# Mixture-of-experts stage: a fixed instruction order on three engines, weight splits four pieces ahead, thirteen packed positions

## The chip, the cores and the metric

One core of one Trainium2 chip runs the whole program in one launch. The metric is the device time of an execution in microseconds (us); less is better.

## What is computed

One layer of a decoder: attention and a convolution side by side, then a mixture of experts, both added to x, and a last norm. The change lies in the mixture of experts. Its core, for 1024 tokens of 1024 values, 32 experts, and two experts to each token:

```python
top_val, top_idx = lax.top_k(e_logits, TOP_K_INNER)
top_w = jax.nn.softmax(top_val, axis=-1) * p_grp[:, None]
...
return (jax.nn.silu(xblk @ w_gate[e]) * (xblk @ w_up[e])) @ w_down[e]
...
x = x + gt2 * hier_moe(h2, ...)
return rms_norm(x, g_final)
```

Everything is float32. Each expert has three weights, gate and up (1024 x 512) and down (512 x 1024), 2 MB each, so 192 MB of weights pass through the core once.

## The kernel before

**Stages.** The first 600 us compute attention, convolution, output projection and router. From about 604 us on, the experts are worked through in 32 positions. Positions 0 to LO-1 (LO = 6) hold the experts 0 to 5; the later positions are filled by the number of tokens of an expert, so that which expert stands at which position is known only when the router is done.

**Positions.** An ordinary position takes up to 128 tokens. A *packed* position (those in `PK`) takes an expert with at most 64 tokens. Position `XP` takes the expert with most tokens, in two blocks; the second is called position 32 (`E`), and each weight piece is used for both. Tokens beyond a position's capacity go to overflow blocks behind position 31, which are skipped when there are none, as here.

**One position.** A gather (L911, issued by GpSimd) fetches the rows of h from memory into one of NX = 3 buffers xe; TensorE transposes them (`stage_x`, L958, packed L949); gate and up follow (`stage_gu`), then a transpose of the hidden values (`stage_h`, L1012, packed L1006), then down (`stage_d`), a scaling on VectorE (packed L1040) and a scatter with addition into memory (L1023, GpSimd).

**Splits.** An ordinary position multiplies in a fast format and gets float32 accuracy from splitting both factors into a high and a low part. Each weight is cut into four pieces of 128 x 1024 values: ScalarE casts one to its high part (L924, ehi), VectorE subtracts (L925, elo), and TensorE does six matmuls (L990 to L992 for gate and up, L1056 to L1058 for down), 24 for a weight. A packed position takes the raw weight in float32 (L970, L1034) without a split. ehi and elo have three buffers each:

```python
hi = moe.tile([P, 2, 512], F32R, name="ehi", bufs=3)
lo = moe.tile([P, 2, 512], F32R, name="elo", bufs=3)
nc.scalar.copy(hi, src)
(nc.gpsimd if i == pool else nc.vector).tensor_tensor(lo, src, hi.bitcast(F32), op=OP.subtract)
```

**The weight stream.** SyncE loads every weight as two DMAs of 1 MB (L597) into a ring of eight slots of 2 MB, in the order of `uses`: gate of e, up of e, down of e-1. A load waits until the last reader of the weight eight places earlier is done. From position LO on, the expert's number is read from `pos` into a register of SyncE (L937) ahead of the first load of that position.

**Order of the work.** The program is written position by position: gate and up of e, transposes for e+1, down of e-1, transposes of e's hidden values. A scheduler of the language reorders the instructions within each engine. In program order the tables of the positions (`position_tables`, from L1097: which expert stands where, which tokens it has, their weights) stand behind position 1; the scheduler put them beside the gate of position 3.

```python
if e == LO - 5:
    position_tables()
```

Of the kernel before, what the change touches and what calls it, by code (L numbers as in the profile page):

```python
# [9 lines left out]
F32 = mybir.dt.float32  # L10
# [23 lines left out]
LO = 6  # L34
XP = 18
PK = (7, 9, 11, 13, 16, 17, 19, 20, 23, 25, 28, 31)
# [4 lines left out]
GUP = None  # L41
DP = None
# [3 lines left out]
def trunk_kernel(ctx, tc, x, c, w_mod, b_mod, g_norm1, w_in, conv_w, conv_b, conv_ln_g, conv_ln_b,  # L46
# [778 lines left out]
    uses = [u for e in range(E + 1) for u in ((e, 0), (e, 1), (e - 1, 2)) if 0 <= u[0] < E]  # L825
    wt = {}
# [32 lines left out]
    half_t = [rtc.tile([P, E - LO], dt, name=f"{nm}h") for nm, dt in (("ti", I32), ("ws", F32))]  # L859
# [8 lines left out]
    def tables(tb, dst, pool, halves=False):  # L868
# [8 lines left out]
        else:  # L877
# [28 lines left out]
    gat = []  # L906

    def gather(e):
        t = xe[len(gat) % NX]
        n = 2 if e in PK else 1  # L910
        i = nc.gpsimd.indirect_dma_start(  # L911
            out=t[:, 0:D // n], out_offset=None, in_=h2d.rearrange("t (n f) -> (t n) f", n=n),
            in_offset=bass.IndirectOffsetOnAxis(ap=slots(e)[0], axis=0),
            bounds_check=n * T - 1, oob_is_err=False)
        gat.append(i)
        return t

    def wparts(w, pool=None):

        for i in range(4):  # L920
            hi = moe.tile([P, 2, 512], F32R, name="ehi", bufs=3)
            lo = moe.tile([P, 2, 512], F32R, name="elo", bufs=3)
            src = w[:, 2 * i:2 * i + 2, :]
            nc.scalar.copy(hi, src)  # L924
            (nc.gpsimd if i == pool else nc.vector).tensor_tensor(lo, src, hi.bitcast(F32), op=OP.subtract)  # L925
            yield i, hi, lo

    st = {}

    expert = {}  # L930

    def stage_w(e):

        for u in uses[len(wt):3 * e + 2]:
            p, i = u
            if p >= LO and p not in expert:
                expert[p] = nc.values_load(pos[0:1, p:p + 1], engines=[mybir.EngineType.SP],  # L937
                                           min_val=0, max_val=E - 1)
            wt[u] = eload(wsrc(p, i, expert.get(p), p in PK))

    def stage_x(e):

        xt = st.pop(("g", e))
        if e in PK:

            x4 = moe.tile([P, 4, P], F32, name="x4", tag="xh")
            pt = psx.tile([P, 4, P], F32, name="pt")
            for j in range(4):
                nc.tensor.transpose(pt[:, j, :], xt[:, j:512:4], ident)  # L949
            nc.scalar.copy(x4, pt)  # L950
            st["x", e] = x4
            return
        xh = moe.tile([P, 8, P], F32R, name="xh")
        xl = moe.tile([P, 8, P], F32R, name="xl")
        for kk in range(2):
# [4 lines left out]
        st["x", e] = xh, xl  # L960

    def gu_halves(e):


        x4 = st.pop(("x", e))
        pg, pu = [psg.tile([P, F], F32, name=nm)[:, 0:256] for nm in ("pg", "pu")]
        for w, o in zip((wt[e, 0], wt[e, 1]), (pg, pu)):
            for k in range(8):
                for c in range(2):
                    nc.tensor.matmul(o[64 * c:64 * c + 64, :], x4[:, k % 4, k // 4 * 64:k // 4 * 64 + 64],  # L970
                                     w[:, k, 256 * c:256 * c + 256], start=(k == 0), stop=(k == 7),
                                     skip_group_check=True)
        hs = moe.tile([P, F], F32, name="hs")[:, 0:256]
        nc.scalar.activation(hs, pg, AF.Silu)
        nc.vector.tensor_mul(hs, hs, pu)
        st["h", e] = hs

    def stage_gu(*es):

        if es[0] in PK:  # L980
            return gu_halves(es[0])
        xs = [st.pop(("x", e)) for e in es]
        ps = []
        for w, nm in zip((wt[es[0], 0], wt[es[0], 1]), ("pg", "pu")):
            p = [psg.tile([P, F], F32, name=nm) for e in es]
            for i, hi, lo in wparts(w, GUP):
                for o, (xh, xl) in zip(p, xs):
                    for kk in range(2):
                        k = 2 * i + kk
                        nc.tensor.matmul(o, xh[:, k, :], hi[:, kk, :], start=(k == 0), stop=False)  # L990
                        nc.tensor.matmul(o, xh[:, k, :], lo[:, kk, :], start=False, stop=False)  # L991
                        nc.tensor.matmul(o, xl[:, k, :], hi[:, kk, :], start=False, stop=(k == 7))  # L992
            ps.append(p)
        for e, pg, pu in zip(es, *ps):
            hs = moe.tile([P, F], F32, name="hs")
            nc.scalar.activation(hs, pg, AF.Silu)
            nc.vector.tensor_mul(hs, hs, pu)
            st["h", e] = hs

    def stage_h(e):  # L1000
        hs = st.pop(("h", e))
        pt = psx.tile([P, 4, P], F32, name="pth")
        if e in PK:

# [3 lines left out]
            nc.scalar.copy(h2, pt[:, 0:2, :])  # L1008
            st["t", e] = h2
            return  # L1010
        for k in range(4):
            nc.tensor.transpose(pt[:, k, :], hs[:, k:F:4], ident)  # L1012
        if e == E:

            hh, hl = [moe.tile([P, 8, P], F32R, name=nm)[:, 0:4, :] for nm in ("xh", "xl")]
        else:
            hh, hl = [moe.tile([P, 4, P], F32R, name=nm, bufs=1) for nm in ("hh", "hl")]
        split(hh, hl, pt)
        st["t", e] = hh, hl

    def scatter(ys, e, n):
# [3 lines left out]
            out_offset=bass.IndirectOffsetOnAxis(ap=slots(e)[0], axis=0),  # L1025
            in_=ys, in_offset=None, bounds_check=n * T - 1, oob_is_err=False, compute_op=OP.add)

    def d_halves(e):
        h2 = st.pop(("t", e))
        wd = wt[e, 2].rearrange("p (k a) f -> p k (a f)", a=2)  # L1030
        py = psx.tile([P, D], F32, name="py")[:, 0:512]
        for k in range(4):
            for g in range(2):
                nc.tensor.matmul(py[64 * g:64 * g + 64, :], h2[:, k % 2, k // 2 * 64:k // 2 * 64 + 64],  # L1034
                                 wd[:, k, 512 * g:512 * g + 512], start=(k == 0), stop=(k == 3),
                                 skip_group_check=True)
        ys = moe.tile([P, D], F32, name="ys")[:, 0:512]
        for g in range(2):
            ps = slice(64 * g, 64 * g + 64)
            nc.vector.scalar_tensor_tensor(ys[ps], py[ps], slots(e)[1][ps], gt2b[ps, 512 * g:512 * g + 512],  # L1040
                                           op0=OP.mult, op1=OP.mult)
        scatter(ys, e, 2)

    def stage_d(*es):
        if es[0] in PK:
            return d_halves(es[0])
        hs = [st.pop(("t", e)) for e in es]
        wd = wt[es[0], 2]
        py = psx.tile([P, D], F32, name="py")
        py = [[py[:, 0:512], py[:, 512:1024]]]  # L1050
        if len(es) > 1:
            py.append([psg.tile([P, F], F32, name=nm) for nm in ("pg", "pu")])
        for k, hi, lo in wparts(wd, DP):
            for (hh, hl), o2 in zip(hs, py):
                for half, o in enumerate(o2):
# [3 lines left out]
        for e, o2 in zip(es, py):  # L1059
            ws = slots(e)[1]  # L1060
            ys = moe.tile([P, D], F32, name="ys")
            for half, o in enumerate(o2):
                sl = slice(half * 512, half * 512 + 512)
                nc.vector.scalar_tensor_tensor(ys[:, sl], o, ws, gt2b[:, sl], op0=OP.mult, op1=OP.mult)  # L1064
            scatter(ys, e, 1)

    def stage_g(e):
        st["g", e] = gather(e)


    order = [e for e in range(E) for e in ((e, E) if e == XP else (e,))]

    def next_x():

        n = nx[0]
        nx[0] += 1
        stage_x(order[n])
        if n + NX < len(order):
            stage_g(order[n + NX])

    nx = [0]

    def pth(p, n):
        return psx.tile([P, 512], F32, name="pth")[0:p, 0:n]
# [12 lines left out]
    def position_tables():  # L1097
# [5 lines left out]
        nc.tensor.matmul(pb, ones, Cc, start=True, stop=True)  # L1103
        kb = tmp(P, E)
        v.scalar_tensor_tensor(kb, pb, float(E), iota[:, 0:E], op0=OP.mult, op1=OP.add)
        pc = pth(E, 1)
        nc.tensor.matmul(pc, Cc, ones[:, 0:1], start=True, stop=True)
        cnt, kc, first, r = [tmp(E, 1) for i in range(4)]
        v.tensor_copy(cnt, pc)
        v.scalar_tensor_tensor(kc, cnt, float(E), tok1[0:E, 0:1], op0=OP.mult, op1=OP.add)  # L1110
        v.tensor_scalar(first, tok1[0:E, 0:1], LO + 0.5, float(P), op0=OP.is_lt, op1=OP.mult)
        m = tmp(E, n)
# [207 lines left out]
```

## Time and profile before

| | |
|---|---|
| median of three executions | 1221.63 us (1220.84 to 1222.86) |
| the profiled execution's own time | 1220.17 us |
| its span, first to last instruction | 1218.4 us |
| mean granted clock of TensorE | 0.952 |
| TensorE busy | 1099.1 us (90%) |
| VectorE busy | 809.3 us (66%) |
| ScalarE busy | 530.8 us (44%) |
| GpSimd busy | 216.4 us (18%) |
| moved by DMA | 292.65 MB, mean 240 GB/s |

The span is what the profile divides into stretches; the execution's own time has 1.8 us more around it. PE is TensorE, PEld its weight loads, DVE is VectorE, ACT ScalarE, POOL GpSimd, SP SyncE and SPq its DMA queue. Busy shares are means over stages that have different limits, so they are read by stretch. The granted clock is a share of TensorE's full clock; the DMA share is the mean busy share of the core's 16 DMA engines. In a group of instructions, x is their count, then come busy time and the mean in ns of one; what stands after the last bar or in brackets is the idle time in front of them, with what ended it.

### The profile page before, as it was taken

The page shows a single profiled execution, that of the slowest core. Times are in us where ns is not written, and L with a number is a line of the kernel's source. Part 1 is how long each engine was busy: PE and PEld are TensorE (multiplying, and loading weights), DVE is VectorE, ACT ScalarE, POOL GpSimd, SP SyncE. Part 2 cuts the span into 40 slices and gives each one's busy share as a digit, 9 for nine tenths or more (in the row PEclk, how much of TensorE's full clock was granted, in tenths as well). Part 3 has the DMA queues.
Part 4 walks back from the last instruction along what each step waited for, and adds up shares of the span by engine and source line. Part 5 has one row for each costly group of instructions (what it writes and reads, how often), then busy time and mean ns, then how long its engine had stood idle before and what let it go on. Part 6 is the DMA issues. An engine that isn't in the chain of part 4 may idle for free. (4 is left out here: it accounts for less than half of the span.)

```text
span 1218.4 us, 15998 instructions
## 1 busy us (share of the span) xinstructions
PE 1099.1 (90%) x5838; PEld 801.9 (66%) x5838; DVE 809.3 (66%) x1320; ACT 530.8 (44%) x809; POOL 216.4 (18%) x205
## 2 busy tenths in 40 slices
PE   4899999998999999999499999999989999999950
PEld 0667777786566666888377787777757666666630
DVE  1458999993664657776588997666743476576633
ACT  2431111114676753332276776555533354464513
POOL 2340000005221105001400222221220112111012
PEclk8799999999998999999699999999999999999985
DMA  9542634202011007745689899999999999999427
GB/s 366 190 156 78 234 108 169 104 1 87 2 35 36 1 2 265 282 155 210 258 293 317 300 355 386 410 407 401 392 379 392 395 389 385 392 383 388 176 49 283
DMA packets 60956, 292.65 MB, mean 240 GB/s; under 512 B 12072, under 2 KB 16424, under 8 KB 33220
## 3 DMA queue, kind: packets, MB, share of 16 engines
q1 hardware_dynamic: 48020, 253.16, 53.5%
q0 software_dynamic: 11424, 34.17, 9.9%
q10 hardware_dynamic: 1424, 4.20, 0.9%
q8 instruction: 48, 0.79, 0.3%
q14 instruction: 40, 0.33, 0.1%
HBM read 276.27 MB, written 26.76 MB: 249 GB/s over the span
## 5 line engine op out<-in xcount | busy, mean ns | idle before, releaser
L925 DVE TENSOR_TENSOR elo<-raw,ehi 128x1024 fp32r<-128x1024 f32 x240 | 286.9, 1222 | 48.2 <-ACT ehi L924 43.7
L924 ACT CAST ehi<-raw 128x1024 fp32r<-128x1024 f32 x240 | 249.1, 1051 | 93.9 <-PE pg L992 41.0
L319 DVE SCALAR_TENSOR_TENSOR cv<-cv,cwT 128x1024 f32<-128x1024 f32 x120 | 154.1, 1284 | 3.6
L271 PE MATMUL pb<-hT,whi 128*128 128x512 f32 x256 | 100.9, 394 | 1.7 <-POOL hT L100 1.3
L270 PE MATMUL pb<-hT,whi 128*128 128x512 f32 x256 | 102.1, 400 | 0.0
L272 PE MATMUL pb<-hT,wlo 128*128 128x512 f32 x256 | 100.4, 393 | 0.0
L991 PE MATMUL pg<-elo,xh 128*128 128x512 f32 x168 | 69.5, 414 | 7.9 <-DVE elo L925 7.9
L990 PE MATMUL pg<-ehi,xh 128*128 128x512 f32 x168 | 69.2, 413 | 5.2 <-ACT ehi L924 4.5
L1023 POOL DMA_INDIRECT x1d<-ys,ti x21 | 38.4, 1828 | 185.1 <-DVE ys L1064 173.6
L1057 PE MATMUL py<-elo,hh 128*128 128x512 f32 x160 | 66.1, 413 | 2.6 <-DVE elo L925 2.6
L991 PE MATMUL pu<-elo,xh 128*128 128x512 f32 x168 | 67.0, 399 | 1.4 <-DVE elo L925 1.4
L992 PE MATMUL pg<-ehi,xl 128*128 128x512 f32 x168 | 68.1, 405 | 0.0
L990 PE MATMUL pu<-ehi,xh 128*128 128x512 f32 x168 | 66.0, 393 | 1.2 <-ACT ehi L924 1.2
L992 PE MATMUL pu<-ehi,xl 128*128 128x512 f32 x168 | 65.5, 390 | 0.0
L1056 PE MATMUL py<-ehi,hh 128*128 128x512 f32 x160 | 65.1, 407 | 0.1
L1058 PE MATMUL py<-ehi,hl 128*128 128x512 f32 x160 | 63.9, 399 | 0.0
L270 PEld LDWEIGHTS pb<-hT,whi 128*128 128x128 f32 x256 | 48.3, 189 | 21.8 <-ACT whi L104 9.2
L271 PEld LDWEIGHTS pb<-hT,whi 128*128 128x128 f32 x256 | 48.2, 188 | 13.1 <-POOL hT L100 2.9
L272 PEld LDWEIGHTS pb<-hT,wlo 128*128 128x128 f32 x256 | 48.2, 188 | 10.4 <-DVE wlo L107 0.6
L424 ACT ACTIVATE ns<-ns,st 128x128 f32<-128x128 f32 (+7 forms) x64 | 49.4, 774 | 11.5 <-DVE st L420 11.1
L911 POOL DMA_INDIRECT xe<-h2d,ti x21 | 26.2, 1249 | 149.8 <-PE pt L958 99.8
L420 DVE CUSTOM_DVE_ANT_0 ns<-sc,raw 128x384 f32<-128x384 f32 (+5 forms) x64 | 33.1, 536 | 27.9 <-PE sc L417 15.7
(284 smaller groups left out, 2225.5 us busy)
## 6 DMA issues: line engine op xcount, KB each, us to landing
raw<-in_w_exp_gate_dram SPq DMA_DIRECT2D x64, 1024.0 KB
raw<-in_w_exp_up_dram SPq DMA_DIRECT2D x64, 1024.0 KB
raw<-in_w_exp_down_dram SPq DMA_DIRECT2D x64, 1024.0 KB
wm<-in_w_mod_dram POOLq DMA_DIRECT2D x16, 1024.0 KB, 5.2
wm<-in_w_mod_dram SPq DMA_DIRECT2D x8, 1024.0 KB
raw<-in_w_in_dram SPq DMA_DIRECT2D x3, 2048.0 KB
xt<-in_x_dram SPq DMA_DIRECT2D x8, 512.0 KB
raw<-in_w_in_dram SPq DMA_DIRECT2D x4, 1024.0 KB
```

The source lines that it names most:

```text
L270: nc.tensor.matmul(p[half], hi[:, k, :], hT[0][:, k, sl], start=(k == 0), stop=False)
L271: nc.tensor.matmul(p[half], hi[:, k, :], hT[1][:, k, sl], start=False, stop=False)
L272: nc.tensor.matmul(p[half], lo[:, k, :], hT[0][:, k, sl], start=False, stop=(k == 7))
L319: nc.vector.scalar_tensor_tensor(y, u[:, j:j + T], w, y, op0=OP.mult, op1=OP.add)
L924: nc.scalar.copy(hi, src)
L925: (nc.gpsimd if i == pool else nc.vector).tensor_tensor(lo, src, hi.bitcast(F32), op=OP.subtract)
L990: nc.tensor.matmul(o, xh[:, k, :], hi[:, kk, :], start=(k == 0), stop=False)
L991: nc.tensor.matmul(o, xh[:, k, :], lo[:, kk, :], start=False, stop=False)
L992: nc.tensor.matmul(o, xl[:, k, :], hi[:, kk, :], start=False, stop=(k == 7))
L1056: nc.tensor.matmul(o, hh[:, k, :], hi[:, half, :], start=(k == 0), stop=False)
L1057: nc.tensor.matmul(o, hh[:, k, :], lo[:, half, :], start=False, stop=False)
L1058: nc.tensor.matmul(o, hl[:, k, :], hi[:, half, :], start=False, stop=(k == 3))
```

## The change

The scheduler no longer orders TensorE, VectorE and ScalarE in this stage: they run in the order written. Pieces are split four ahead of their use (`split_next` behind each piece's six matmuls), with four buffers for ehi and elo in place of three. Other small work (scalings, transposes, table steps) waits in a list `todo`, and `tick` does one entry behind each piece. LO is 4, XP 17, and thirteen positions are packed, in turn from 4 to 20. XP's second block takes 64 tokens (capacity 192 instead of 256) and runs like a packed position, from the raw weight. There are two gather buffers instead of three. The tables are cut into steps by `yield`, and these are done behind the pieces of positions 0 and 1; what they multiply on TensorE goes to the one buffer py. The last four loads are gate of 31, down of 30, up of 31, down of 31.

```diff
-LO = 6
-XP = 18
-PK = (7, 9, 11, 13, 16, 17, 19, 20, 23, 25, 28, 31)
+LO = 4
+XP = 17
+PK = (4, 6, 8, 10, 12, 14, 16, 18, 20, 23, 25, 28, 31)
...
+    uses[-3:-1] = uses[-2], uses[-3]
...
-    NX = 3
-    xe = [mhp.tile([P, D], F32, name=f"xe{i}", tag=f"qk{2 + i}") if i < 2 else moe.tile([P, D], F32, name=f"xe{i}", bufs=1)
-          for i in range(NX)]
+    NX = 2
...
+    def load_to(u):
+
+        for p, i in uses[len(wt):uses.index(u) + 1]:
             if p >= LO and p not in expert:
                 expert[p] = nc.values_load(pos[0:1, p:p + 1], engines=[mybir.EngineType.SP],
                                            min_val=0, max_val=E - 1)
-            wt[u] = eload(wsrc(p, i, expert.get(p), p in PK))
-
-    def stage_x(e):
+            wt[p, i] = eload(wsrc(p, i, expert.get(p), p in PK))
...
+    NP = 4
+    pieces = [(u, j) for u in uses if u[0] not in PK for j in range(4)]
+
+    def split_w(u, j):
+        hi = moe.tile([P, 2, 512], F32R, name="ehi", bufs=NP)
+        lo = moe.tile([P, 2, 512], F32R, name="elo", bufs=NP)
+        split(hi, lo, wt[u][:, 2 * j:2 * j + 2, :])
+        parts[u, j] = hi, lo
+
+    def split_next():
+        if pieces:
+            u, j = pieces.pop(0)
+            load_to(u)
+            split_w(u, j)
...
+    def tick():
+
+        if todo:
+            todo.pop(0)()
+
+    def flush():
+        while todo:
+            tick()
...
+    def products(u, mm, last=None):
+        for j in range(4):
+            if u[0] > E:
+                split_w(u, j)
+            mm(j, *parts.pop((u, j)))
+            if j == 3 and last:
+                last()
+            if u[0] < E:
+                split_next()
+            yield
+
+    def run(g):
+        for _ in g:
+            tick()
...
+    def gate_up(e, i):
+
+
+        u = e, i
+        o = st["o", e, i] = psg.tile([P, F], F32, name=("pg", "pu")[i])
+        if e in PK or e == E:
+            w = wt[XP if e == E else e, i]
...
+    def hidden(e, n=F):
+        hs = st["h", e][:, 0:n]
+        v.tensor_mul(hs, hs, st.pop(("o", e, 1))[:, 0:n])
+        st.pop(("o", e, 0))
...
+        todo.extend([lambda: scale(0), lambda: scale(1)])
 
     def pth(p, n):
-        return psx.tile([P, 512], F32, name="pth")[0:p, 0:n]
+        return psx.tile([P, D], F32, name="py")[0:p, 0:n]
...
         pb = pth(P, E)
         nc.tensor.matmul(pb, ones, Cc, start=True, stop=True)
+        yield
...
             pt = pth(E, 4 * P)
             for a in range(4):
                 nc.tensor.matmul(pt[:, a * P:a * P + P], tb[:, a, q, :], ident, start=True, stop=True)
+            yield
             v.tensor_copy(tT[:, q], pt.rearrange("e (a s) -> e a s", a=4))
...
-        by_position(0, 0, n, [t[:, 0:n] for t in late_t])
-        by_position(1, XP - LO, XP - LO + 1, [t[:, n:n + 1] for t in late_t])
-        by_position(0, 0, n, half_t, True)
+        yield from by_position(0, 0, n, [t[:, 0:n] for t in half_t], True)
+        yield from by_position(0, 0, n, [t[:, 0:n] for t in late_t])
+        x = XP - LO
+        yield from by_position(1, x, x + 1, [t[:, n:n + 1] for t in late_t])
+        yield from by_position(1, x, x + 1, [t[:, n:n + 1] for t in half_t], True)
...
+    with tc.manual_schedule(engines={mybir.EngineType.PE, mybir.EngineType.DVE, mybir.EngineType.Activation}):
+        for n in range(NP):
+            split_next()
+        for f in steps(0):
+            f()
+        table = position_tables()
+        for e in range(E):
+            load_to((e, 0))
+            if e < 2:
+                todo.extend([lambda: next(table, None)] * 8)
+            run(both(gate_up, e, 0))
+            if e == E - 1:
+                load_to((e - 1, 2))
+                run(both(down, e - 1))
+            load_to((e, 1))
+            run(both(gate_up, e, 1))
+            flush()
+            if e == 1:
+                run(table)
+            nxt = steps(e + 1) if e + 1 < E else []
+            if 0 < e < E - 1:
+                load_to((e - 1, 2))
+                nxt.pop(0)()
+                for n, _ in enumerate(both(down, e - 1)):
+                    if nxt and n >= 1 + (e - 1 not in PK):
+                        nxt.pop(0)()
+            for f in nxt:
+                f()
+            tasks = [turn(e)]
+            if e == XP:
+                tasks.append(lambda: todo.insert(0, turn(E)))
+            todo.extend(tasks)
+        flush()
+        load_to((E - 1, 2))
+        for _ in down(E - 1):
+            pass
+        flush()
...
-        c[:, n + E - LO + e - LO] = 64 if e in PK else 256 if e == XP else P
+        c[:, n + E - LO + e - LO] = 64 if e in PK else 192 if e == XP else P
```

**TensorE at the tables.** Before, in position 3's gate (ident and tb are the identity and the router's table, pth a PSUM buffer):

```order
L990 MATMUL pg<-ehi,xh 128x512
L991 MATMUL pg<-elo,xh 128x512
L992 MATMUL pg<-ehi,xl 128x512
L1137 MATMUL pth<-ident,tb 32x128 x4
L990 MATMUL pg<-ehi,xh 128x512
L991 MATMUL pg<-elo,xh 128x512
L992 MATMUL pg<-ehi,xl 128x512
L990 MATMUL pg<-ehi,xh 128x512
L1137 MATMUL pth<-ident,tb 32x128 x4
L991 MATMUL pg<-elo,xh 128x512
L992 MATMUL pg<-ehi,xl 128x512
```

Now, in the up projection of position 0 (L1024 to L1026 are the products that were L990 to L992, L1178 was L1137):

```order
L1168 MATMUL py<-ys,cs 1x28
L1169 MATMUL py<-ones,caps 1x1
L1024 MATMUL pu<-ehi,xh 128x512
L1025 MATMUL pu<-elo,xh 128x512
L1026 MATMUL pu<-ehi,xl 128x512
L1024 MATMUL pu<-ehi,xh 128x512
L1025 MATMUL pu<-elo,xh 128x512
L1026 MATMUL pu<-ehi,xl 128x512
L1178 MATMUL py<-ident,tb 32x128 x4
```

The table's matmuls stand behind whole pieces of six products; before, they stood within them. Six further products and the second L1178 follow.

**VectorE at the same place.** Before:

```order
L1130 TENSOR_SCALAR pos<-pth 1x26
L1131 CAST pos<-pth 1x1
L925 TENSOR_TENSOR elo<-raw,ehi 128x1024
L1138 COPY ys<-pth 32x512
L925 TENSOR_TENSOR elo<-raw,ehi 128x1024
L1138 COPY ys<-pth 32x512
L925 TENSOR_TENSOR elo<-raw,ehi 128x1024
L1149 COPY ys<-pth 128x104
```

Now (L105 is the subtraction of every split, L1180 was L1138):

```order
L105 TENSOR_TENSOR elo<-raw,ehi 128x1024
L1171 TENSOR_SCALAR pos<-py 1x28
L1172 CAST pos<-py 1x1
L1038 TENSOR_TENSOR hs<-hs,pu 128x512
L105 TENSOR_TENSOR elo<-raw,ehi 128x1024
L1180 COPY ys<-py 32x512
L105 TENSOR_TENSOR xl<-pt,xh 128x512 x2
L105 TENSOR_TENSOR elo<-raw,ehi 128x1024
L105 TENSOR_TENSOR hl<-pth,hh 128x512
L105 TENSOR_TENSOR elo<-raw,ehi 128x1024
L1180 COPY ys<-py 32x512
```

Each read of py stands behind the subtraction of the split that was asked for with it; three subtractions of the input's and the hidden values' splits stand between the two copies.

**TensorE at the end.** Before, the last rows with a product (x and h are the inputs of packed positions):

```order
L1058 MATMUL py<-ehi,hl 128x512
L970 MATMUL pg<-raw,x_9312 64x256 x16
L970 MATMUL pu<-raw,x_9312 64x256 x16
L1006 MATMUL pth<-ident,hs 128x128 x2
L1056 MATMUL py<-ehi,hh 128x512
```

Twenty-three more products of the down projection of position 30 and then position 31's, L1034, follow. Now:

```order
L1101 MATMUL py<-ehi,hl 128x512
L1014 MATMUL pu<-raw,x_9234 64x256 x16
L1058 MATMUL pth<-ident,hs 128x128 x2
L1082 MATMUL py<-raw,h_9384 64x512 x8
```

The down projection of position 30 has moved in front of the up projection of position 31; the down projection of 31 ends both.

## Rows read from the trace of the kernel before

**Rows 1.** Stretches of the span: us, busy time of each engine, PEclk, DMA share, GB/s.

```profile
core 0: us, PE busy (x) PEld busy (x) DVE busy (x) ACT busy (x) POOL busy (x), PEclk, DMA share, GB/s
625.00:685.00 60.00, 58.67 (x298) 46.64 (x297) 53.18 (x82) 40.88 (x46) 7.57 (x5) 1.00 0.87 298
741.00:800.00 59.00, 59.00 (x339) 42.03 (x339) 41.88 (x45) 32.18 (x39) 12.78 (x8) 1.00 1.02 397
911.00:1125.00 214.00, 200.14 (x1035) 142.33 (x1036) 127.54 (x134) 98.76 (x120) 34.75 (x22) 0.98 1.01 389
1140.00:1150.00 10.00, 10.00 (x38) 7.82 (x37) 7.15 (x7) 6.32 (x8) 0.00 (x0) 0.84 0.43 126
1150.00:1160.00 10.00, 10.00 (x55) 7.80 (x55) 7.42 (x9) 4.27 (x5) 0.00 (x0) 1.00 0.00 0
```

**Rows 2.** Waits of SyncE: released by, us in total, times, longest us.

```profile
SPq L597 <- DVE elo L925: 150.2, 67, 11.3
...
SPq L597 <- DMA raw<-in_w_exp_gate_dram: 80.1, 37, 3.5
```

**Rows 3.** Timeline of SyncE, expert loads: start us, us, the instructions in one run.

```profile
662.19 4.74 SPq L597 DMA_DIRECT2D raw<-in_w_exp_down_dram  x2
675.73 2.51 SPq L597 DMA_DIRECT2D raw<-in_w_exp_gate_dram  x2
...
802.44 2.06 SPq L597 DMA_DIRECT2D raw<-in_w_exp_down_dram  x2
...
1103.54 2.06 SPq L597 DMA_DIRECT2D raw<-in_w_exp_down_dram  x2
```

**Rows 4.** Timeline of TensorE at the starts of positions and the last product.

```profile
603.77 1.11 PE L958 MATMUL pt<-ident,xe 128*128 128x128 f32 x4 [6.81 <-DMA xe<-h2d,ti]
...
685.73 0.39 PE L990 MATMUL pg<-ehi,xh 128*128 128x512 f32 x1
685.96 0.39 PE L991 MATMUL pg<-elo,xh 128*128 128x512 f32 x1
...
704.28 0.48 PE L990 MATMUL pg<-ehi,xh 128*128 128x512 f32 x1
...
741.00 3.67 PE L970 MATMUL pg<-raw,x 128*64 128x256 f32 x32
...
770.74 3.67 PE L970 MATMUL pg<-raw,x 128*64 128x256 f32 x32
...
1174.31 3.65 PE L1034 MATMUL py<-raw,h 128*64 128x512 f32 x16 [1.55 <-issue]
```

**Rows 5.** Waits of TensorE between 911 and 1178 us.

```profile
PE pg L991 <- DVE elo L925: 7.9, 8, 1.8
PE pg L990 <- ACT ehi L924: 4.5, 4, 1.6
```

**Rows 6.** TensorE in the old table stretch: us, busy (x), clock, DMA share, GB/s.

```profile
661.00:673.00 12.00, 12.00 (x79) 1.00 0.76 269
```

**Rows 7.** Groups by line between 600 and 741 us: the splits.

```profile
L925 DVE TENSOR_TENSOR elo<-raw,ehi 128x1024 fp32r<-128x1024 f32 x81 | 97.2, 1221 | 9.5 <-ACT ehi L924 7.7
L924 ACT CAST ehi<-raw 128x1024 fp32r<-128x1024 f32 x80 | 83.9, 1051 | 34.6 <-PE pg L992 15.8 <-PE py L1058 7.5 <-PE pu L992 5.9
```

**Rows 8.** Timeline of VectorE: a copy of the old table stretch.

```profile
662.64 0.68 DVE L1138 COPY ys<-pth 32x512 f32<-32x512 f32 x1 [0.48 <-PE pth L1137]
```

**Rows 9.** Stretches as in rows 1, where the granted clock falls.

```profile
990.00:993.00 3.00, 1.53 (x8) 0.83 (x7) 2.48 (x3) 3.00 (x5) 2.10 (x2) 1.00 0.99 392
993.00:996.00 3.00, 2.78 (x7) 2.20 (x8) 2.44 (x3) 1.02 (x2) 0.53 (x1) 0.52 1.01 406
```

**Rows 10.** Timeline of all engines at the end: the last scatters.

```profile
1174.48 1.55 POOL L1023 DMA_INDIRECT x1d<-ys,ti  x1 [12.74 <-DVE ys L1064]
...
1178.00 1.51 DVE L1040 SCALAR_TENSOR_TENSOR ys<-py,wsh,gt2b 64x512 f32<-64x512 f32 x2 [3.79 <-PE py L1034]
...
1186.65 1.57 POOL L1023 DMA_INDIRECT x1d<-ys,tih  x1 [10.61 <-issue]
```

More of the change, by code (lines that the diff above doesn't have):

```diff
@@ L978, in stage_gu @@
[L978 to L998, printed above, removed]
@@ L1000, in stage_h, with mm @@
-    def stage_h(e):
+                    nc.tensor.matmul(o[64 * c:64 * c + 64, 0:256], x(k), w[:, k, 256 * c:256 * c + 256],
+                                     start=(k == 0), stop=(k == 7), skip_group_check=True)
+                if k % 2:
+                    yield
+        else:
+            xh, xl = st["x", e]
+            def mm(j, hi, lo):
+                for kk in range(2):
+                    k = 2 * j + kk
+                    nc.tensor.matmul(o, xh[:, k, :], hi[:, kk, :], start=(k == 0), stop=False)
+                    nc.tensor.matmul(o, xh[:, k, :], lo[:, kk, :], start=False, stop=False)
+                    nc.tensor.matmul(o, xl[:, k, :], hi[:, kk, :], start=False, stop=(k == 7))
+            yield from products(u, mm, (lambda: hidden(e)) if i else None)
@@ L1001, in stage_h, with turn @@
+        if i == 0:
+            hs = st["h", e] = moe.tile([P, F], F32, name="hs")
+            n = 256 if e in PK or e == E else F
+            nc.scalar.activation(hs[:, 0:n], o[:, 0:n], AF.Silu)
+        elif e in PK or e == E:
+            hidden(e, 256)
+    def hidden(e, n=F):
+        hs = st["h", e][:, 0:n]
+        v.tensor_mul(hs, hs, st.pop(("o", e, 1))[:, 0:n])
+        st.pop(("o", e, 0))
+    def turn(e):
         hs = st.pop(("h", e))
         pt = psx.tile([P, 4, P], F32, name="pth")
+        if e == E:
+            for k in range(4):
+                for c in range(2):
+                    cs = slice(64 * c, 64 * c + 64)
+                    nc.tensor.matmul(pt[cs, k, 0:64], hs[cs, k:256:4], ident[cs, cs], start=True, stop=True,
+                                     skip_group_check=True)
+            h2 = moe.tile([P, 4, 64], F32, name="h2e", bufs=1)
+            st["t", e] = lambda k: h2[:, k, :]
+            return lambda: nc.scalar.copy(h2, pt[:, :, 0:64])
@@ L1018, in stage_h, with scatter @@
-        split(hh, hl, pt)
-        st["t", e] = hh, hl
-    def scatter(ys, e, n):
+        hh, hl = st["t", e] = [moe.tile([P, 4, P], F32R, name=nm, bufs=1) for nm in ("hh", "hl")]
+        return lambda: split(hh, hl, pt)
+    def scatter(ys, si, n):
         nc.gpsimd.indirect_dma_start(
             out=x1d.rearrange("t (n f) -> (t n) f", n=n),
-            out_offset=bass.IndirectOffsetOnAxis(ap=slots(e)[0], axis=0),
+            out_offset=bass.IndirectOffsetOnAxis(ap=si, axis=0),
             in_=ys, in_offset=None, bounds_check=n * T - 1, oob_is_err=False, compute_op=OP.add)
[L1028 to L1055, printed above, removed]
+    def down(e):
+        t = st.pop(("t", e))
+        if e in PK or e == E:
+            wd = wt[XP if e == E else e, 2].rearrange("p (k a) f -> p k (a f)", a=2)
+            py = psg.tile([P, F], F32, name="pg") if e == E else psx.tile([P, D], F32, name="py")[:, 0:512]
+            for k in range(4):
+                for g in range(2):
+                    nc.tensor.matmul(py[64 * g:64 * g + 64, :], t(k), wd[:, k, 512 * g:512 * g + 512],
+                                     start=(k == 0), stop=(k == 3), skip_group_check=True)
+                yield
+            o2 = [(slice(64 * g, 64 * g + 64), slice(0, 512), py[64 * g:64 * g + 64, :],
+                   slice(512 * g, 512 * g + 512)) for g in range(2)]
+            if e == E:
+                si, ws = [t[:, E - LO:E - LO + 1] for t in half_t]
+            else:
+                si, ws = slots(e)
+            w, n = 512, 2
+        else:
+            hh, hl = t
+            py = psx.tile([P, D], F32, name="py")
+            halves = [py[:, 0:512], py[:, 512:1024]]
+            def mm(k, hi, lo):
+                for half, o in enumerate(halves):
@@ L1058, in stage_d, with scale @@
                     nc.tensor.matmul(o, hl[:, k, :], hi[:, half, :], start=False, stop=(k == 3))
[L1059 to L1081, printed above, removed]
+            yield from products((e, 2), mm)
+            o2 = [(slice(0, P), slice(512 * i, 512 * i + 512), o, slice(512 * i, 512 * i + 512))
+                  for i, o in enumerate(halves)]
+            si, ws = slots(e)
+            w, n = D, 1
+        ys = moe.tile([P, D], F32, name="ys")[:, 0:w]
+        def scale(i):
+            ps, sl, o, gl = o2[i]
+            v.scalar_tensor_tensor(ys[ps, sl], o, ws[ps], gt2b[ps, gl], op0=OP.mult, op1=OP.mult)
+            if i:
+                scatter(ys, si, n)
+        todo.extend([lambda: scale(0), lambda: scale(1)])
     def pth(p, n):
-        return psx.tile([P, 512], F32, name="pth")[0:p, 0:n]
+        return psx.tile([P, D], F32, name="py")[0:p, 0:n]
     class Scratch:
@@ L1238, in overflow @@
                 wt[e, i] = eload(wsrc(e, i, eid), slot=2 + i)
-            for f in (stage_g, stage_x, stage_gu, stage_h, stage_d):
-                f(e)
+            gather(e)
+            for f in x_steps(e):
+                f()
+            for g in (gate_up(e, 0), gate_up(e, 1)):
+                for _ in g:
+                    pass
+            turn(e)()
+            for _ in down(e):
+                pass
+            flush()
             if j + 1 < NOV:
```

135 lines of the change are left out of this document (64 added, 71 removed).

## The prediction, made before the changed kernel was run

> **What bounds the kernel now.** I read the stage table first. From 741 to 1125 us the DMA engines are full: their share is 1.02 and 1.01, at 397 and 389 GB/s, while TensorE is busy 59.00 of 59.00 and 200.14 of 214.00 us [rows 1]. In 625:685 the share is 0.87, and it falls to 0.43 in 1140:1150 and to 0.00 in 1150:1160, so the last expert weight lands at about 1150. Then SyncE's waits: 150.2 us, in 67 waits, for VectorE's subtraction L925, that is, for a ring slot to come free, and 80.1 us, in 37 waits, for earlier gate loads to land [rows 2]. So the stream of weights is held by slots early and by the DMA engines later. Its pace when full comes from two issues of whole tiles, 802.44 and 1103.54 [rows 3]: by the order of loads they are tiles 40 and 91 of 0 to 95 (a tile is one weight, 2 MB), so 301.1 us / 51 = 5.90 us a tile, with the gathers and scatters that fall between.
>
> Next, TensorE's positions. An unpacked position (three weights of 24 matmuls, 0.23 us from one start to the next) takes 704.28 - 685.73 = 18.55 us; an unpacked and a packed one take 770.74 - 741.00 = 29.74, so a packed one takes 11.2 [rows 4]. Two packed-unpacked positions need 6 x 5.90 = 35.4 us of DMA: from the first packed position on, TensorE can be faster than the weights, and what is left of the time is mostly the stream. Yet the kernel does not end with the stream: the last down projection is finished at 1177.96 (1174.31 + 3.65 [rows 4]), 28 us after the last weight. Between 911 and 1178 TensorE waits for casts and subtractions, 7.9 and 4.5 us at the first matmuls of a gate [rows 5], and runs in part at the low clock.
>
> **The change, part by part.** I call t4 the start of position 4's gate, which becomes the first packed one (before it was position 7), and T the landing of the last weight. Before, t4 was 685.73.
>
> *Tables.* This is where the change costs. Before, the position tables stood in position 3's gate (661 to 673), and TensorE was busy 12.00 of 12.00 us there [rows 6]: the scheduler had put one or two matmuls behind each small copy. Now they stand in positions 0 and 1, each step directly behind a piece of six matmuls. A step's TensorE part needs VectorE's part of the same step, since all share the one py buffer or read its result. That VectorE part stands behind the next split, whose cast needs the buffer of the piece just multiplied. So TensorE goes through: last matmul of the piece, cast 1.05, subtraction 1.22 [rows 7], own operations 0.5 to 1.4 by their number (the copy of 32x512 takes 0.68 [rows 8]; the small ones are taken at 0.2 to 0.3 each, an estimate from it), then on. The order shows eight such steps (L1143, L1168, L1178 twice, L1187, L1189 twice, L1187 again). Priced one by one: 2.8, 3.3, 2.9, 3.3, 3.7, 2.9, 2.9, 2.9 = 24.7; position 1's second four transposes wait for the first half's cast and subtraction, 1.4. Together 26 us. The nearest row for the lower bound is the old stretch, which shows nothing lost; I take 26, since the order leaves no freedom.
>
> *Start to t4.* First transposes at 603.77, as before [rows 4]. To t4 lie eleven weights of 24 x 0.233 = 5.6 us (61.6), transposes of some 7, table matmuls 3, 2 for the first ten matmuls at the lower clock (an estimate: 0.23 us more on each), and 1.7 because both halves of position 0's input now come before its first product: 679. With the 26 it is 705. Splits four pieces ahead keep TensorE fed otherwise: twelve subtractions at 1.22 = 14.7 us of VectorE [rows 7] fit into the 18.55 of a position.
>
> *The clock.* [...] I take half, 8: t4 = 713. [...]
>
> *Splits early.* Slots come free about one weight earlier, and all twelve waits for a cast at a gate's start (12.4 us [rows 5]) go, since pieces are split while the weight before is multiplied. What is late next is the weight itself.
>
> *One position more packed, position 18's second 128 tokens now 64.* TensorE: 18.55 - 11.2 = 7.4 us less, and some 6 for the extra block; VectorE: twelve splits fewer. All of it lies beside the stream, so nothing on the path. From t4, 15 x 18.55 + 13 x 11.2 + 12 for the extra 64 tokens = 436 us of TensorE against 458 of stream: 22 us of cover. Gathers and scatters shrink by about 1 MB, 2 to 3 us at 390 GB/s; taken as 0, the pace above having its own such errors.
>
> *SyncE.* All 28 position registers and the overflow count are now read in one row, between tiles 10 and 11, 29 reads; before, six lay between the issues at 662.19 + 4.74 and 675.73, 8.8 us with the slot's wait [rows 3], so at most 1.5 us each. By the count above the positions are known at about 628, so the reads end by 672 at the latest; tiles 11 to 18 then need 8 x 5.9 = 47 us, to 719, against 715, when tile 18 must be there: 0 to 4 us, taken 0, since part of the 8.8 was a wait. GpSimd: gathers two ahead instead of three; each still has two positions, over 25 us.
>
> *Stream.* At t4 a full ring of eight tiles reaches to tile 18; tile 19 goes into the slot that position 4's gate frees after 3.7 us (half of a packed gate and up), and 77 tiles follow at 5.90: T = 713 + 3.7 + 454.3 = 1171.0.
>
> *End.* The new order of the last loads puts down of 30 before up of 31. Scatters go one after the other: before, at 1174.48 and 1186.65, 12.2 apart, though VectorE's scaling for the second began at 1178.00 [rows 10]. Now down of 30 ends about 3.8 us before T (its weight lands two tiles earlier, then 2.3 for cast and subtraction and 5.6 for 24 matmuls), its scatter goes at T - 1.5, the last at T + 10.7. TensorE itself ends near T + 5, so the scatters are the later ones. From the last scatter to the end it was 1218.4 - 1186.65 = 31.75 us. Span = 1171.0 + 42.5 = 1213.5, and with the 1.8 us that lay around the profiled span (1220.17 against 1218.4) 1215.3. I forecast **1215**. The profiled execution lay 1.5 under the median of 1221.63; I leave that in the range.
>
> **The rivals.**
> [...]
> 2. *The clock stays up*: t4 = 705, 1207. Against it: the fall itself [rows 9].
> 3. *The table steps are hidden*: if the casts run ahead of the step after all, t4 is 685 as before, and the time 1187. For it: the stretch without a loss [rows 6]. Against it: the order of VectorE, copy behind subtraction.
> 4. *TensorE stays behind the stream* in the second half by the 28 us it has now, because waits move from the casts to the copies of x and h, which stand behind casts for weights that have not landed: T + 28 + 40.4 + 1.8 = 1241. For it: 13 changes between packed and unpacked; against: 22 us of cover.
>
> **How the numbers follow.** Chances: forecast 0.42, rivals 0.18, 0.18, 0.12 and 0.10 in their order. A difference of 0.2% (2.4 us) is about what a measurement of this kernel can tell from none: 1219.2 to 1224.1 is the same. The forecast's own range is 1208 to 1224 (t4 by 5 either way, the pace by 0.04): 0.31 faster, 0.06 same, 0.05 slower. Rivals 2 and 3 are faster, 0.30, less 0.03 for their tail; rival 1 gives 0.06 same and 0.12 slower, rival 4 slower. Sum 0.58, 0.14 and 0.28. The range goes from 1195, half way to rival 3, to 1230, past rival 1, and leaves out rival 4 and most of rival 3.
>
> **What would show it.** Right: TensorE's start of position 4's gate at 705 to 721, with waits of some 3 us for VectorE before L1143, L1168, L1178, L1187 and L1189 and a clock below 1.00 between 621 and 670; a DMA share of 1.00 from about 730 to T; TensorE ending within 8 us of T; two last scatters 12 us apart. Wrong: t4 under 695 (the steps are hidden), a DMA share clearly under 1.00 after 750 (slots, not the engines, hold the stream), or TensorE over 15 us behind the last weight (rival 4).

## The result, and the profile after

The changed kernel takes **1235.77 us** (median of four, 1232.49 to 1237.52), against 1221.24 for the kernel before in the same comparison: a ratio of 1.012, 95% interval 1.0089 to 1.0151. The forecast was 1215, faster, with a range of 1195 to 1230. The time lies outside it, on the other side.

The profiled execution took 1232.49, its span is 1230.7. The forecast's own landmarks, t4 (the start of position 4's gate) and T (the landing of the last weight), read from it:

| | forecast | before | after |
|---|---|---|---|
| t4 | 713 | 685.7 | 720.7 |
| T - t4 | 458.0 | | 464.0 |
| T | 1171.0 | about 1150 | 1184.7 |
| end of the last product | T + 5 | T + 28 | T + 11.9 |
| end of the span | T + 42.5 | T + 68 | T + 46.0 |
| the profiled execution | 1215.3 | 1220.17 | 1232.49 |

T is the issue of the last MB of weights plus its time to landing; for after both rows are shown below. For before the profile gives no landing; there T is read from the DMA share, 0.43 in 1140:1150 and 0.00 in 1150:1160 [rows 1], so it and what is counted from it are rounded. The stretches that answer to [rows 1], and one at the end (us, busy time of each engine with its instructions, granted clock, DMA share, GB/s):

```profile
core 0: us, PE busy (x) PEld busy (x) DVE busy (x) ACT busy (x) POOL busy (x), PEclk, DMA share, GB/s
625.00:685.00 60.00, 41.75 (x169) 31.37 (x169) 22.79 (x41) 16.62 (x19) 1.98 (x2) 0.62 0.32 107
741.00:800.00 59.00, 59.00 (x342) 42.61 (x341) 39.79 (x43) 31.45 (x39) 12.49 (x8) 1.00 1.02 407
911.00:1125.00 214.00, 198.94 (x1105) 142.21 (x1106) 135.24 (x143) 107.34 (x130) 41.98 (x26) 0.96 1.00 387
1150.00:1160.00 10.00, 8.95 (x44) 5.47 (x42) 8.50 (x9) 5.79 (x8) 2.31 (x1) 1.00 0.97 344
```

Between 625 and 685 TensorE is now busy 41.75 us where it was 58.67, the granted clock is 0.62 where it was 1.00, and the stream runs at a share of 0.32 where it ran at 0.87: SyncE issues 6 loads of 1 MB where it issued 17, and they wait for VectorE, whose subtractions free ring slots [rows 2], up to 13.5 us where they waited up to 4.9. From 741 on everything looks nearly as before. At 1150 to 1160, where the stream had ended before, it is still full (0.97).

In the stretch with the loss, the waits of TensorE between 600 and 690 us (waiting line, released by, us in total, times, longest; the line for the 6.8 us ahead of the first transposes, as before, is left out):

```profile
PE py L1189 <- DVE ys L1192: 5.3, 2, 2.7
PE py L1169 <- DVE caps L1166: 4.0, 1, 4.0
PE py L1187 <- DVE ys L1180: 3.3, 1, 3.3
PE py L1178 <- DVE ys L1180: 3.1, 1, 3.1
PE pt L994 <- DVE xl L105: 2.8, 2, 1.4
PE py L1187 <- DVE ys L1192: 2.6, 1, 2.6
PE py L1178 <- DVE pos L1172: 2.5, 1, 2.5
PE py L1143 <- DVE ys L1141: 2.5, 1, 2.5
PE py L1168 <- DVE ys L1155: 0.5, 1, 0.5
```

Without the line for L994 these are the table steps: 23.8 us (forecast 24.7), at the lines that the forecast named and L1169 beside L1168. The longest of them on the timeline of all engines:

```profile
619.27 0.39 PE L1026 MATMUL pu<-ehi,xl 128*128 128x512 f32 x1
...
620.15 0.21 PE L1168 MATMUL py<-ys,cs 32*1 32x28 f32 x2 [0.49 <-DVE ys L1155]
620.90 1.23 DVE L105 TENSOR_TENSOR elo<-raw,ehi 128x1024 fp32r<-128x1024 f32 x1 [0.80 <-ACT ehi L102]
...
622.88 1.20 DVE L105 TENSOR_TENSOR elo<-raw,ehi 128x1024 fp32r<-128x1024 f32 x1
...
624.19 0.15 DVE L1166 TENSOR_REDUCE caps<-ys 32x1 f32<-32x8 f32 x1
624.40 0.18 PE L1169 MATMUL py<-ones,caps 32*1 32x1 f32 x2 [4.04 <-DVE caps L1166]
624.51 0.80 PE L1024 MATMUL pu<-ehi,xh 128*128 128x512 f32 x1
```

TensorE stands still for 4.04 us, because a reduction of 0.15 us (L1166) stands on VectorE behind two subtractions of 1.2 us for pieces that TensorE needs only later. A product shows 0.39 us ahead of the pause and 0.63 behind it (L1025 and L1026 from 625.11 on). The stretch around it, in TensorE's busy time, clock, DMA share and GB/s:

```profile
620.00:630.00 10.00, 3.27 (x11) 0.62 0.63 210
630.00:640.00 10.00, 6.93 (x24) 0.50 0.18 48
640.00:650.00 10.00, 6.53 (x24) 0.69 0.24 87
650.00:660.00 10.00, 6.07 (x34) 0.65 0.28 105
660.00:670.00 10.00, 5.87 (x17) 0.50 0.30 106
```

In two of these stretches the clock is at 0.50, in the others at 0.62 to 0.69. The end of the kernel, from the timelines of TensorE, SyncE and GpSimd, in order of time:

```profile
720.69 3.67 PE L1014 MATMUL pg<-raw,x 128*64 128x256 f32 x32
...
1161.20 2.81 SPq L595 DMA_DIRECT2D raw<-in_w_exp_down_dram  x2
...
1187.36 0.39 PE L1101 MATMUL py<-ehi,hl 128*128 128x512 f32 x1
...
1189.47 1.55 POOL L1069 DMA_INDIRECT x1d<-ys,ti  x1 [5.97 <-DVE ys L1112]
...
1192.91 3.65 PE L1082 MATMUL py<-raw,h 128*64 128x512 f32 x16 [0.46 <-ACT h L1061]
...
1198.59 1.57 POOL L1069 DMA_INDIRECT x1d<-ys,tih  x1 [7.57 <-DVEq L1322]
```

The DMA issues after 1160 us (KB each, median us to landing):

```profile
raw<-in_w_exp_down_dram SPq DMA_DIRECT2D x2, 1024.0 KB, 21.0
```

The last half of the last weight is issued at 1161.20 + 2.81 - 0.33 = 1163.7 (an issue takes 0.33) and lands 21.0 later: T = 1184.7. The last product ends at 1192.91 + 3.65 = 1196.56. The last scatter goes 9.1 us behind the one before and 2 us behind the last product.

### The profile page after: what moved, and what is told of

Same layout as the page of the kernel before. It is cut to its first block, busy times and chain, and to the rows that moved or that the text cites. A ratio compares the mean times of both kernels' runs of the same rounds, so it can differ in the third digit from the quotient of the medians.

```text
span 1230.7 us, 16064 instructions
## 1 busy us (share of the span) xinstructions
PE 1088.1 (88%) x5876; PEld 795.1 (65%) x5876; DVE 790.8 (64%) x1307; ACT 517.1 (42%) x795; POOL 223.2 (18%) x204
## 5 line engine op out<-in xcount | busy, mean ns | idle before, releaser
L105 DVE TENSOR_TENSOR elo<-raw,ehi 128x1024 fp32r<-128x1024 f32 x228 | 273.3, 1223 | 113.9 <-ACT ehi L102 110.0
L102 ACT CAST ehi<-raw 128x1024 fp32r<-128x1024 f32 x228 | 237.9, 1049 | 159.6 <-PE pg L1026 55.5
L1024 PE MATMUL pg<-ehi,xh 128*128 128x512 f32 x152 | 64.0, 421 | 0.0
L1038 DVE TENSOR_TENSOR hs<-hs,pu 128x512 f32<-128x512 f32 (+1 forms) x33 | 18.9, 572 | 69.2 <-PE pu L1014 64.3
L1024 PE MATMUL pu<-ehi,xh 128*128 128x512 f32 x152 | 62.4, 410 | 0.0
L1025 PE MATMUL pu<-elo,xh 128*128 128x512 f32 x152 | 61.6, 405 | 0.0
L1026 PE MATMUL pu<-ehi,xl 128*128 128x512 f32 x152 | 61.5, 405 | 0.0
L1025 PE MATMUL pg<-elo,xh 128*128 128x512 f32 x152 | 61.4, 404 | 0.0
L1026 PE MATMUL pg<-ehi,xl 128*128 128x512 f32 x152 | 61.3, 403 | 0.0
L1100 PE MATMUL py<-elo,hh 128*128 128x512 f32 x152 | 59.6, 392 | 0.0
L1101 PE MATMUL py<-ehi,hl 128*128 128x512 f32 x152 | 59.5, 391 | 0.0
L1014 PE MATMUL pg<-raw,x 128*64 128x256 f32 x448 | 56.4, 408 | 0.0
## 6 DMA issues: line engine op xcount, KB each, us to landing
raw<-in_w_in_dram SPq DMA_DIRECT2D x4, 1024.0 KB, 11.9
```

The lines of the kernel that those rows point to most:

```text
L105: nc.vector.tensor_sub(lo, src, hi.bitcast(F32))
L1100: nc.tensor.matmul(o, hh[:, k, :], lo[:, half, :], start=False, stop=False)
L1101: nc.tensor.matmul(o, hl[:, k, :], hi[:, half, :], start=False, stop=(k == 3))
```

## The experiments

**Theory S**: the loss is TensorE's wait for small VectorE operations that stand behind the next split, with the low clock that follows (0.60 between 621 and 680); T then follows t4 at a fixed distance. **Rival N**: the stream and the fixed order (two gather buffers, changes between packed and unpacked positions) set the time whatever happens in positions 0 and 1. **Rival P**: the packed positions from the 4th on do. All ratios are to the kernel before, with their 95% intervals.

**e1: the table step ahead of the split, in positions 0 and 1 alone.**

```diff
+            if u[0] < 2 and u[1] < 2:
+                yield
             if u[0] < E:
                 split_next()
-            yield
+            if not (u[0] < 2 and u[1] < 2):
+                yield
```

> Only the order within positions 0 and 1 differs from the changed kernel: a table step is written ahead of the next split instead of behind it. Theory S (the loss is TensorE's wait for a small VectorE operation that stands behind the next split, with the low clock that follows): a step's wait falls from 2.5-3.3 us to about 1.5, eight times, so position 4's gate starts near 708 instead of 720.7 and the time is about 1223. Rival N (the time is set by the stream and the fixed order whatever happens in positions 0 and 1): within 3 us of 1235.8.

Measured: 1205.26 us, 0.987 (0.9836 to 0.9904). Position 4's gate starts at 696.0, T is 1160.7. A reordering of two lines takes 30 us off the median. The profiled executions differ by 23.3 (1209.21, the slowest of e1's four, against 1232.49, the quickest of the changed kernel's) and T by 24.0. It is more than S expected, since the waits fell further than I had worked out; the waits of the table steps that are left:

```profile
PE py L1172 <- DVE caps L1169: 2.6, 1, 2.6
PE py L1190 <- DVE ys L1183: 1.6, 1, 1.6
PE py L1181 <- DVE ys L1183: 1.5, 1, 1.5
PE py L1146 <- DVE ys L1144: 0.2, 1, 0.2
```

**e2: the steps also cut, so that no matmul follows the operation that it needs directly.**

```diff
...
+        yield
+        yield
         pp = pth(1, E + 1)
...
+        pt = pth(E, 8 * P)
         for q in range(2):
-            pt = pth(E, 4 * P)
...
+        yield
+        yield
...
+        pt = pth(P, 8 * (n + 1))
+        for o, (q, c0, c1, dst, halves) in zip(at, jobs):
...
```

> The table steps stand ahead of the split and are cut so that TensorE's part of a step comes at least one whole piece behind the VectorE operation that it needs, and its small matmuls are gathered in four places. Theory S: the 24 us of waits in positions 0 and 1 go, and with them some 13 us of low clock; position 4's gate starts at about 684, the last weight lands near 1148 and the time is about 1199, faster than both kernels. Rival N: the time stays above 1225, because something else in the fixed order (two gather buffers, the change between packed and unpacked positions) holds the stream.

Measured: 1198.11 us, 0.9822 (0.9784 to 0.986). Position 4's gate starts at 687.5, T is 1151.7, the span 1196.3. All waits of TensorE between 600 and 730:

```profile
PE pt L997 <- DMA xe<-h2d,ti: 6.7, 1, 6.7
PE pt L997 <- DVE xl L105: 5.1, 2, 3.7
PE py L1102 <- ACT ehi L102: 0.7, 1, 0.7
```

Not one wait of a table step is left, and the time is 37.7 us under the changed kernel's, as S expected (1199). Rival N falls.

**e3: the changed kernel, with products of no use in the waits.**

```diff
+    def fill():
+        xh, xl = st["x", cur[0]]
+        d = psx.tile([P, 4, P], F32, name="pth")
+        for i in range(10):
+            nc.tensor.matmul(d, xh[:, i % 8, :], xl[:, 0:4, :], start=True, stop=True)
...
```

> The changed kernel with ten products of no use put on TensorE ahead of each table matmul that waits (twenty at the longest wait), so that the array works through the wait; their results are not read. Theory S with the clock as its own term: the waits stay but are filled, the granted clock between 621 and 680 goes from about 0.6 to near 1.0, position 4's gate starts at about 707 and the time is about 1222. If the clock has no part in it: position 4's gate at 721 or later, 1236 or more.

Measured: 1217.42 us, 0.9975 (0.9955 to 0.9994). Position 4's gate starts at 708.4. TensorE in stretches, and one fill (L1138) with the table's matmuls behind it on the timeline:

```profile
620.00:640.00 20.00, 17.44 (x89) 1.00 0.48 158
640.00:660.00 20.00, 17.46 (x95) 1.00 0.35 117
```

```profile
626.42 2.43 PE L1138 MATMUL pth<-xl,xh 128*128 128x512 f32 x10
629.13 1.06 PE L1190 MATMUL py<-ident,tb 128*32 128x128 f32 x8 [0.28 <-DVE pos L1183]
```

The order of VectorE is unchanged, but the clock is 1.00 between 621 and 680 in place of 0.60, and position 4's gate starts 12.3 us earlier (720.7 to 708.4); the medians differ by 18.4, the profiled execution, 1221.63, being the slowest of e3's ten. The eight matmuls that took 1.91 in the changed kernel take 1.06. The 12.3 us are less than the clock's share: e3 starts 1.2 us later (602.90 for 601.65), and its fills and the waits left over take some 29 us up to t4, where the waits of the changed kernel take 26.6. Outside fills and waits TensorE takes 92.4 us from the first transposes to t4 in the changed kernel and some 76.5 in e3, 16 less. Between the changed kernel and e2 the 33.2 us at t4 divide into 20.8 of waiting (26.6 to 5.8) and 13.5 of TensorE's time outside its waits (92.4 to 78.9, at a clock of 0.60 and 0.94 between 621 and 680), less the 1.1 us by which e2 starts later.

**e4: the changed kernel with the old constants.**

```diff
-LO = 4
-XP = 17
-PK = (4, 6, 8, 10, 12, 14, 16, 18, 20, 23, 25, 28, 31)
+LO = 6
+XP = 18
+PK = (7, 9, 11, 13, 16, 17, 19, 20, 23, 25, 28, 31)
```

> The fixed order with the old constants: LO 6, XP 18 and the twelve packed positions from the 7th on (the second block of XP still takes 64 tokens). Theory S: the table steps cost the same, the stream runs at the pace of the unpacked positions until position 7, 6.2 us a tile instead of 5.9, and the time is 1232 to 1242. Rival P (the packed positions from the 4th on are what holds the stream): 1222 or less.

Measured: 1233.45 us, 1.0098 (1.0063 to 1.0134); T is 1186.7. The same loss, so it is not the packing's.

**e8: e2 with the old constants.** The edit is e4's:

```diff
-LO = 4
...
+LO = 6
...
```

> The kernel with spread table steps and the old constants: LO 6, XP 18, twelve packed positions from the 7th on. Theory S, in which the packing lies beside the stream: 1195 to 1205. Rival P (with the table waits gone, packing from the 4th position on gains what the stream loses on unpacked positions): 1210 or more.

Measured: 1200.82 us, 0.9857 (0.9838 to 0.9876); T is 1149.6. Rival P falls here as well: one more packed position and an earlier start of them are worth 2.7 us between the medians, inside the intervals.

**e5: e2 with the old order at the end**, up of 31 loaded and multiplied ahead of down of 30.

```diff
-    uses[-3:-1] = uses[-2], uses[-3]
...
-            if e == E - 1:
-                load_to((e - 1, 2))
-                run(both(down, e - 1))
...
```

> The kernel with spread table steps (1198.1), and the last loads and products in the old order: up of 31 before down of 30. Theory S and its end (TensorE, not the weights, sets the end: it finishes about 12 us behind the last weight in either order, and two scatters go one after the other 12 us apart): down of 30 is scaled only 4 us before down of 31, so the last scatter moves some 8 us back: 1202 to 1208. Rival: the order of the last loads has no part in it, 1196 to 1200.

Measured: 1205.81 us, 0.9892 (0.9873 to 0.9912), 7.7 above e2; T is 1151.7 as in e2. The last scatters:

```profile
1159.60 1.55 POOL L1071 DMA_INDIRECT x1d<-ys,ti  x1 [6.24 <-DVE ys L1114]
1171.67 1.57 POOL L1071 DMA_INDIRECT x1d<-ys,tih  x1 [10.52 <-issue]
```

They stand 12.1 apart again, as in [rows 10].

**e10: the kernel before, with the loads alone swapped.**

```diff
+    uses[-3:-1] = uses[-2], uses[-3]
```

> The kernel before with one line of the change: down of 30 is loaded ahead of up of 31. Its scheduler keeps TensorE's order, up of 31 ahead of down of 30. If the gain at the end of the fixed order comes from the order of products and the shorter backlog of TensorE, the loads alone bring nothing: 1217 to 1225. Rival (the order of loads is the gain): 1208 to 1214.

Measured: 1219.27 us, 1.0003 (0.9982 to 1.0023). The order of the loads does nothing without the order of the products.

**e7: e2 with positions 26 and 30 packed in place of 25 and 28.**

```diff
-PK = (4, 6, 8, 10, 12, 14, 16, 18, 20, 23, 25, 28, 31)
+PK = (4, 6, 8, 10, 12, 14, 16, 18, 20, 23, 26, 30, 31)
```

> The kernel with spread table steps, and packed positions 26 and 30 in place of 25 and 28, so that positions 30 and 31 are both packed. If TensorE's backlog at the end (12 us behind the last weight) is made by the unpacked positions 29 and 30, it ends about 4 us behind the last weight and the time is about 1191. Rival (the scatters or the norm set the end): 1196 to 1200.

Measured: 1197.58 us, 0.982 (0.9806 to 0.9835): the rival. TensorE does end earlier, at 1158.4 for 1161.7 in e2, 2.9 us behind T = 1155.5, which is itself 3.8 later than in e2. But now the scatters are the row that ends last:

```profile
1147.55 1.55 POOL L1072 DMA_INDIRECT x1d<-ys,ti  x1 [9.22 <-DMA x1d<-ys,ti]
1157.18 1.55 POOL L1072 DMA_INDIRECT x1d<-ys,tih  x1 [8.09 <-DMA x1d<-ys,ti]
1164.97 1.57 POOL L1072 DMA_INDIRECT x1d<-ys,tih  x1 [6.24 <-issue]
```

Two of them are released by the landing of an earlier scatter into the same tensor.

**e9: e2 with 26 and 29 packed.**

```diff
-PK = (4, 6, 8, 10, 12, 14, 16, 18, 20, 23, 25, 28, 31)
+PK = (4, 6, 8, 10, 12, 14, 16, 18, 20, 23, 26, 29, 31)
```

> The kernel with spread table steps, and packed positions 26 and 29 in place of 25 and 28. In the run with 26 and 30 TensorE ended 3 us behind the last weight, but three scatters stood in a row, 8 to 10 us apart. With 29 packed instead, the scatter of 29 is out earlier, TensorE ends some 6 us behind the last weight, and two scatters are left in the row: 1192 to 1196. Rival (the scatters' row or the last weight moves back by as much as TensorE gains): 1197 to 1200.

Measured: 1203.36 us, 0.9873 (0.9846 to 0.9901). A miss on both sides: TensorE ends at 1167.6, 14.3 behind T = 1153.3. Position 29's product ends near 1140, but VectorE scales it at 1147.42 only. The trace shows what stands ahead of it: the subtractions for down of 30, whose casts ScalarE could begin only at 1139.76 and 1143.46, after waiting 7.61 and 1.72 us for that weight to land. TensorE waits 6.34 us, until 1146.42, for hidden values (hs) that stand behind them too. No run changes that order.

**e6: e2 with splits three pieces ahead.**

```diff
-    NP = 4
+    NP = 3
```

> The kernel with spread table steps, splits three pieces ahead in three buffers instead of four. If the fourth piece ahead is beside the stream, as the prediction had all of the split waits: within 3 us of 1198.1. Rival (the fourth buffer is what lets TensorE run through, and so where the fixed order gains): 1205 or more.

Measured: 1204.96 us (1198.19 to 1208.72), 0.9867 (0.9838 to 0.9896), which overlaps e2's interval. So both once more, side by side (e11 is e2 unchanged, e12 is e6).

> The kernel with spread table steps and four buffers once more, on the same chip as the one with three, because the times of the one with three reached from 1198 to 1209 and overlap: 1196 to 1201.

> Splits three pieces ahead in three buffers, on the same chip as the one with four. In the first profile position 4's gate began 5.4 us later than with four, so if the fourth piece ahead counts in positions 0 to 3: 4 to 8 us above the kernel with four. If it lies beside the stream: within 2 us of it.

Measured: e11 1199.12 us, 0.9837 (0.9795 to 0.9878); e12 1202.35, 0.9866 (0.9828 to 0.9904). Position 4's gate starts at 687.0 and 690.3. e11 came out as expected; e12 lies 3.2 us above it, between its two forecasts. The fourth piece seems to be worth some 3 us, before position 4, but the intervals overlap in both pairs: inconclusive.

## Why the prediction was wrong

It named the mechanism and its places, but summed a loss of 21 us (T) and a gain of 26 (the end) to a small gain, and all three terms of the sum were too small by a little: t4 by 7.7, T - t4 by 6.0, the end by 3.5. These are the 17.2 us between 1215.3 and the profiled 1232.49; the median lies 3.3 higher still. The step that failed first is the 8 us for the clock, the author's estimate, a term that no run shows: with the 2 for the first products the runs showed some 19 in its place, as worked out below. The pace of the tiles and the end of TensorE, at T + 5, failed beside it.

**The tables (26 us): right.** The steps' waits are 23.8 us. "The order leaves no freedom" held, and rival 3, hidden steps, is out for the written order. e1 shows that the cause is that order, copy behind subtraction.

**"I take half, 8: t4 = 713": mis-sized.** Start and waits came out 3.2 us better than forecast (601.65 for 603.77, and 26.6 for 27.7 with the waits for x). The loss lies in the clock. Outside its waits TensorE takes 92.4 us up to t4. The forecast had 71.6 at a clock of 1.00 (61.6, 7 and 3) and 2 + 8 for the low clock, 81.6 together and 10.8 less than measured. In e3, with the clock at 1.00 between 621 and 680, the same time is some 76.5, and about 3 of it are lost on the first transposes and products, which run slower there too (an estimate from the starts of the products, 0.43 us apart for 0.23, at a clock of 0.74 in 601:620). So the low clock cost some 19 us where 10 were allowed, and the terms at a clock of 1.00 were short by about 2.

"Table matmuls 3" was too small in either run: the ten groups sum to 10.3 us in the trace (1.91 and 1.89 for L1178, 1.87 and 1.84 for L1189, 0.65 and 1.02 for L1187, 1.1 for the rest), and to 6.5 in e3.

Rival 1, the clock low all through the stretch, did not come true either: the clock is 0.69 in 640:650. The forecast's sign of being right, t4 at 705 to 721, was met by 720.7, which has the 3.2 us of better start and waits in it, though the forecast's own sum passes the old median from 719 on: that sign could not tell faster from slower.

The trace shows slow products behind the waits: of the eight bursts of products that follow a table step's wait of 2.5 us or more, seven begin with products of 0.63 to 0.80 us, and one begins with products of 0.40 to 0.50 (from 651.84) and goes to 0.63 within the burst (at 653.14).

**"77 tiles follow at 5.90": mis-sized.** T - t4 is 464.0, 464.7, 464.2 and 464.2 in after, e1, e2 and e3, against 458. Two issues of whole tiles, 40 and 91 as in [rows 3], are 1135.10 - 831.40 = 303.7 us apart in after, 5.955 a tile; over 77 tiles that is 4.2 of the 6; the other 1.8 are not placed. The count began as forecast: the second half of tile 19 is issued at 724.4, 3.7 us behind t4. Why a tile takes 0.05 longer was not tried. That T follows t4 at one distance is the sturdiest thing in the forecast: e2 and after differ by 33.2 at t4 and by 33.0 at T.

**"TensorE itself ends near T + 5": wrong.** It ends at T + 11.9, and the last scatter waits for it. The forecast let the last weights set the pace there, with down of 30 done 3.8 us before T. It is done at 1187.36 + 0.39 = T + 3.1, and from 1150 on TensorE has no wait above 1.1 us: it is behind the weights and does not wait for the last of them. Positions 29 and 30 are both unpacked; e7, which packs 30, ends at T + 2.9. The forecast's two scatters 12 apart are 9.1 apart. In e7 the row of scatters, the forecast's own bound, does set the end.

**Splits early, SyncE, packing: right.** SyncE's reads hold nothing up: tile 18 is issued at 714.78, before t4. The waits of a gate's first matmuls [rows 5] are gone between 911 and 1178; what TensorE waits for there is new, the hidden values (hs), which stand on VectorE behind splits of weights that have not landed, rival 4's mechanism (ahead of the wait of 8.8 us, which ends at 914.78, ScalarE waited 10.99 us for down of an expert to land):

```profile
PE pth L1063 <- DVE hs L1038: 16.8, 2, 8.8
PE pt L994 <- DVE xl L105: 3.2, 3, 1.1
PE pt L981 <- DVE xl L105: 1.2, 1, 1.2
```

The DMA share of 1.00 in that stretch shows that they are covered. Packing lies beside the stream, as e4 and e8 show.

**Where the expected gain went.** The change does gain, all of it behind T: before, the span ended about 68 us after T, in e2 44.6. T itself is 1151.7 in e2 and about 1150 before. The changed kernel has this gain too (46.0), and gives about 35 us back at T, for steps whose operations take 0.15 to 0.7 us. Of the roughly 23 us in e2, 7.7 are the order of the last loads and products together (e5); how the rest divides between the fixed order, the early splits and the shorter second block of XP was not tried.

## What to carry to other kernels

Where a fixed order replaces a scheduler, look for small operations that another engine waits for and that stand behind a long one that nobody waits for: write the small one first, and put the waiting instruction a whole unit of work later. Price such a stretch, small matmuls included, at a granted clock measured beside pauses of its kind: here 0.60 between 621 and 680, where the filled waits of e3 had 1.00. When a forecast is the small difference of two large terms, the range must take in the errors of both: here each term was within 10 us and the sign still came out wrong.

## What was not expected of the hardware

Products whose results nobody reads shortened the kernel: 1217.42 for 1235.77 us, with the clock between 621 and 680 at 1.00 in place of 0.60. And scatters with addition into the same tensor followed each other at 7.8, 9.6 (e7) and 12.1 us (e5), though the later one's input was scaled some 5 to 7 us before it went; the last of them went 6.6 us (e7) and 8.6 us (e5) behind the end of TensorE's last product.
